# Another starting place for the low parts of the weights, and another pair of distances in each feed-forward stage

## The chip, the core and the metric

The kernel runs on one core of a Trainium2 chip. The metric is the device time of one execution in microseconds (us). A core has TensorE (PE in the profile; its weight loads have a row of their own, PEld), VectorE (DVE), ScalarE (ACT), GpSimd (POOL) and SyncE (SP, which here only issues DMAs). A matmul holds a block of 128x128 weights in the array and streams the other operand past it; the load of the next block runs while the present operand streams. Both are read from SBUF, which has 128 partitions. In each partition, every operand is a run of 4-byte elements that begins at some address.

## What is computed

A decoder trunk of two layers on 256 tokens of width 1024, all in 32-bit floats:

```python
h = x
for layer in range(2):
    if layer == 1:
        shared_kv = shared_moba_kv(h, positions, kv_norm_g, w_kv, k_norm_g)
    h = h + 0.5 * swiglu(rms_norm(h, ffn1_norm_g[layer]), w_gate, w_up, w_down)   # stages a and c
    hn = rms_norm(h, mix_norm_g[layer])
    # layer 0: convolution module beside attention to a memory
    # layer 1: causal attention over shared_kv beside attention to a memory
    ...
    h = h + jnp.concatenate([primary, mem_out], axis=-1) @ w_o[layer]
    h = h + 0.5 * swiglu(rms_norm(h, ffn2_norm_g[layer]), w_gate2, w_up2, w_down2)  # stages b and d

def swiglu(x, w_gate, w_up, w_down):
    return (jax.nn.silu(x @ w_gate) * (x @ w_up)) @ w_down
```

The inner width of a feed-forward stage is 2816, that is 22 tiles of 128.

## The kernel before

Activations are held transposed: features on the partitions, the 256 tokens along the free dimension. For the sake of precision each 32-bit operand is split into a high part, which TensorE takes at full speed, and the low part that is left over. A product is then three: high by high, high by low and low by high.

Weights come from HBM in chunks of 128x2048, each worked in two halves of 128x1024 (eight blocks of 128x128). `half_hi` gives each half two buffers out of a ring of four: ScalarE copies the high part into `wh`, VectorE writes the low part into `wl` (the raw weights less the high part). Each `wh` and each `wl` buffer is 1024 elements long.

The activations of a stage lie in one buffer from `y_tiles(name, at)`. It is 128 elements longer than its content, and the content begins `at` elements into it. For each of the eight feature tiles k the high part (256 elements) is followed by the low part (256). The numbers `at` come from the table `Y_AT` and are 8 where nothing else is said.

A feed-forward stage (`ffn`, four calls: a, b, c, d) has two halves. The **gate half** goes over 22 tiles j, and for each over gate and up and over eight k (tiles named `ag`, `au`, `bg` and so on): 352 pairs of matmuls. The **down half** goes over eight output tiles m and 22 k (tiles `ao`, `bo` and so on). Its moving operand is `hs`, the product of the gate half, in high and low parts laid out as in `y`. Both use `mm2`, a pair of matmuls on one k: a **wide** one with the block of `wh` as its weights, which streams high and low part together (512 columns), and a **narrow** one with the block of `wl`, which streams the high part alone (256 columns). The last output tile of the down half uses `mm3`, three narrow matmuls per k (`wh`, `wh` again, `wl`), so a down half has 7 x 22 = 154 pairs and 66 single narrow ones. In stage a the first two tiles j are taken together: per k four wide matmuls, then four narrow ones, eight such blocks in all.

While the wide matmul of k streams, the next load is that block of `wl`; while the narrow one streams, the next load is the `wh` block of the following k. What is called **distance** here is the start of the streaming operand less the start of the block being loaded, in elements of 4 bytes, counted modulo 32 (128 bytes). As the buffers are laid out, `y`, `wh` and `wl` buffers all begin at the same place modulo 128 bytes, and `hs` begins 8 elements further. All steps inside them (128 elements from block to block, 512 from k to k) are multiples of 32. So a `y` that begins 8 elements into its buffer has distance 8 from `wh` and from `wl`, and `hs` has distance 8 from both too.

Other products in the program have other distances. The projections `kv`, `A`, `B`, `C`, `M` and `mkv` stream weights 512 columns wide past activations with `at` 0 (distance 0). `Q` does so with 256 columns (distance 0). `mqJ`, `b0J`, `b1J` and `b2J` stream weights 256 columns wide past `cy`, which has `at` 16 (distance 16). `obo` streams `cat` 256 columns wide past blocks of `wh` and `wl` (distance 8).

Of the kernel before, what the change touches and what calls it, by code (L numbers as in the profile page):

```python
# [10 lines left out]
F32R = mybir.dt.float32r  # L11
# [6 lines left out]
P = 128  # L18
DM = 1024
KD = DM // P  # L20
SEQ = 256
NT = SEQ // P
DFF = 2816
KF = DFF // P
# [14 lines left out]
HC = 1024  # L39
# [69 lines left out]
S_A, S_B, S_BIAS, S_F, S_G = 0, PW, 2 * PW, 3 * PW, 3 * PW + P  # L109
NSPEC = 4 * PW  # L110

Y_AT = {"ay0": 0, "by0": 0, "cy0": 16}

@with_exitstack
def tile_kernel(ctx: ExitStack, tc: tile.TileContext, w, xT, memT, pos, vec, hg, const, wave, bias, taps, out):
    nc = tc.nc
    cp = ctx.enter_context(tc.tile_pool(name="cp", bufs=1))
    wp = ctx.enter_context(tc.tile_pool(name="wp", bufs=3))
# [32 lines left out]
    nc.vector.memset(mhalf, -0.5)  # L151


    state = {"chunk": 0, "half": 0, "raw": None, "order": "", "last": {}, "between": None, "made": []}

    def behind(i, other):
        tc.add_manual_dep(i.ins, other.ins.name,
# [20 lines left out]
    def tables(func):  # L178

        behind(A(nc.scalar.activation(warm, onec, func)), state["func"])  # L180
# [10 lines left out]
    def load_chunk(n):  # L191
        if n == 0:
            return raw0
        raw = wp.tile([P, CH], F32, name=f"raw{n}", tag="raw", bufs=3)
        if n < 3:
            nc.sync.dma_start(raw[:, :HC], w[n][:, :HC])
            state["sync"] = nc.sync.dma_start(raw[:, HC:], w[n][:, HC:])
        else:
            state["sync"] = nc.sync.dma_start(raw, w[n])
        return raw  # L200

    def half_hi():
        n, h = state["chunk"], state["half"]
        if h == 0:
            state["raw"] = load_chunk(n)
        raw = state["raw"][:, h * HC:(h + 1) * HC]
        wh = wp.tile([P, HC], F32R, name=f"wh{n}_{h}", tag="wh", bufs=4)
        wl = wp.tile([P, HC], F32R, name=f"wl{n}_{h}", tag="wl", bufs=4)
        state["chunk"], state["half"] = (n, 1) if h == 0 else (n + 1, 0)
        q = HC // 2 if n < 2 else HC  # L210
        parts = [slice(c, c + q) for c in range(0, HC, q)]

        def hi(s):
            state["act"] = nc.scalar.activation(wh[:, s], raw[:, s], AF.Copy)  # L214
            return state["act"]

        def lo(s):
            state["dve"] = nc.vector.tensor_tensor(wl[:, s], raw[:, s], wh[:, s].bitcast(F32), op=ALU.subtract)  # L218
            return state["dve"]
        return wh, wl, parts, hi, lo  # L220

    def half_chunk():
        if state["made"]:
            return state["made"].pop(0)
        wh, wl, parts, hi, lo = half_hi()
        for s in parts:
            hi(s)
            lo(s)
        return wh, wl

    def tiles_of(n_half):
        for n in range(n_half):
            wh, wl = half_chunk()
            for i in range(8):
                yield wh[:, i * P:(i + 1) * P], wl[:, i * P:(i + 1) * P]

    def mm3(o, wt, y, k, first, last, **kw):
        h, l = wt
        i = mmul(o, h, y[:, k, 0], start=first, stop=False, **kw)
        mmul(o, h, y[:, k, 1], start=False, stop=False, **kw)  # L240
        mmul(o, l, y[:, k, 0], start=False, stop=last, **kw)
        return i

    def mm2(o, wt, y, k, first, last, turn=None):

        h, l = wt
        a = mmul(o, h, y[:, k].rearrange("p a s -> p (a s)"), start=first, stop=False)
        if turn is not None:
            state["between"] = a
            turn()  # L250
            last_turn, state["between"] = state["between"], None
        b = mmul(o[:, :SEQ], l, y[:, k, 0], start=False, stop=last)
        if turn is not None:
            behind(b, last_turn)
# [9 lines left out]
    def both_halves(name, o, tag):  # L264

        c = tp.tile([P, SEQ], F32, name=name + "c", tag="cvq")
        nc.scalar.activation(c, o[:, SEQ:], AF.Copy)
        a = tp.tile([P, SEQ], F32, name=name, tag=tag)
        nc.vector.tensor_tensor(a, o[:, :SEQ], c, op=ALU.add)
        return a  # L270
# [7 lines left out]
    def psum(name, tag="mm", bufs=4):  # L278
        return ps.tile([P, 512], F32, name=name, tag=tag, bufs=bufs)


    def y_tiles(name, at=8):

        n = KD * 2 * SEQ
        y = yp.tile([P, n + P], F32R, name=name, tag="y")
        return y[:, at:at + n].rearrange("p (k h s) -> p k h s", k=KD, h=2)

    def scaled_split(y, src, k, g, on_dve=False):

        yh, yl = y[:, :, 0], y[:, :, 1]  # L290
        if on_dve:
            h = nc.vector.tensor_scalar(yh[:, k], src, vt[:, g + k:g + k + 1], None, op0=ALU.mult)
        else:
            h = nc.scalar.activation(yh[:, k], src, AF.Copy, scale=vt[:, g + k:g + k + 1])
        return h, nc.vector.scalar_tensor_tensor(yl[:, k], src, vt[:, g + k:g + k + 1], yh[:, k].bitcast(F32),
                                                 op0=ALU.mult, op1=ALU.subtract)

    def square_sum(name, acc, src, first, adder=nc.gpsimd):
        if first:
            nc.scalar.activation(acc, src, AF.Square)  # L300
        else:
            sq = tp.tile([P, SEQ], F32, name=name, tag="sq")
            nc.scalar.activation(sq, src, AF.Square)
            adder.tensor_tensor(acc, acc, sq, op=ALU.add)
# [32 lines left out]
    def new_acc(name):  # L337
        return tp.tile([P, SEQ], F32, name=name, tag="acc")

    def ffn(name, y, acc, nexts, store=False, hook=None, after=None, hook_down=None, r=None, plan=None):  # L340


        plan = plan or {}
        rows_at = [j for (j, _, _), what in plan.items() if what == "rows"]
        hs = cp.tile([P, KF, 2, SEQ], F32R, name=name + "hs", tag="hs")
        first = acc is None
        rb = None if r is None else bcast_rows(name + "nb", r)
        halves = {}
# [22 lines left out]
        for j in range(KF):  # L371
# [4 lines left out]
            if first and j == 0:  # L376
# [21 lines left out]
                n = KD  # L398
# [9 lines left out]
            else:  # L408

                at = ("sc", 2) if first and j == 2 else ()  # L410
# [21 lines left out]
            for i in sorted(halves):  # L432
                g, h = halves.pop(i)
                if i > 1 or not rows_at:
                    g, h = both_halves(f"{name}gs{i}", g, "g"), (lambda i=i, h=h: both_halves(f"{name}h{i}", h, "h"))
                gated(i, g, h, rb)
        if after:
            tables(after)
        ys = [y_tiles(f"{name}y{i}", Y_AT.get(f"{name}y{i}", 8)) for i in range(len(nexts))]
        acc = new_acc(name + "acc")  # L440
        it = tiles_of(KD * KF // 8)
        for m in range(KD):
            po = psum(f"{name}o{m}")
            if hook_down:
                with tc.issue_after(state["act"].ins):
                    hook_down(m)

            both_sums = m < KD - 1
            for k in range(KF):
                if both_sums:  # L450
                    mm2(po, next(it), hs, k, k == 0, k == KF - 1)
                else:
                    mm3(po[:, :SEQ], next(it), hs, k, k == 0, k == KF - 1)
            if both_sums:
                d = both_halves(f"{name}d{m}", po, "g")
                nc.vector.scalar_tensor_tensor(d, d, 0.5, rb, op0=ALU.mult, op1=ALU.mult)
            else:
                d = tp.tile([P, SEQ], F32, name=f"{name}d{m}", tag="g")
                nc.vector.scalar_tensor_tensor(d, po[:, :SEQ], 0.5, rb, op0=ALU.mult, op1=ALU.mult)
            nc.vector.tensor_tensor(x[:, m], d, x[:, m], op=ALU.add)  # L460
            if store:
                nc.sync.dma_start(out[m], x[:, m])
                continue
            for yy, g in zip(ys, nexts):
                state["ends"] = scaled_split(yy, x[:, m], m, g)
            square_sum(f"{name}q{m}", acc, x[:, m], m == 0)
        return ys, acc

    def heads_norm(name, t, n):
# [78 lines left out]
    def room_of(tile_):  # L548

        taken = [0]  # L550

        def place(*shape):

            n = int(np.prod(shape))
            taken[0] += n
            assert taken[0] <= tile_.shape[1], taken
            piece = tile_[:, taken[0] - n:taken[0]]
            if len(shape) == 1:
                return piece
            names = [f"d{i}" for i in range(len(shape))]  # L560
            return piece.rearrange(f"p ({' '.join(names)}) -> p {' '.join(names)}", **dict(zip(names, shape)))
        return place
# [143 lines left out]
        square_sum(f"{name}q{m}", acc, x[:, m], m == 0)  # L706


    y = y_tiles("y0")
    for k in range(KD):  # L710
        scaled_split(y, x[:, k], k, V_FFN1, k % 2 == 0)
    kv0 = []
# [416 lines left out]
        steps[name]()  # L1129
    state["order"] = ""  # L1130
    o, cat = late["o"], late["cat"]
    ys = y_tiles("oay")
    acc = new_acc("oaacc")
    it = tiles_of(CC - FIRST_CAT)
    for m in range(KD):
        for k in range(FIRST_CAT, CC):
            mm3(o[m], next(it), cat, k, False, k == CC - 1, skip_group_check=True)
        out_end(m, o, ys, acc, V_FFN2, "oa")
    y = ys
    (ykv, y), acc = ffn("b", y, acc, (V_KV, V_FFN1 + KD), plan={(2, "g", 5): "rows"})  # L1140


# [11 lines left out]
                    plan={(2 + i, "g", 4): turn for i, turn in enumerate(turns)})  # L1154
    qT = cp.tile([P, KD, SEQ], F32, name="q1T", tag="t8k")
    cat = y_tiles("cat1")
    ys = y_tiles("oby")
    place = room_of(cp.tile([P, KF * 2 * SEQ], F32, name="room", tag="hs"))
    steps, step = stepper()

# [186 lines left out]
    y, acc = ys, sums  # L1347
# [162 lines left out]
```

## Time and profile before

| what | value |
|---|---|
| median of three runs | 958.7 us (958.36 to 959.63) |
| the profiled execution, its time | 958.8 us |
| its span, first to last instruction | 956.8 us |
| PE busy | 950.2 us, 99% of the span |
| DVE, ACT, POOL busy | 75%, 59%, 11% |
| HBM read | 172.15 MB, 181 GB/s over the span |
| granted TensorE clock | 1.000 |

The span is one execution as the profiler recorded it; its time holds 2.0 us more that lie around the span. A row of the timeline gives the start, the duration, engine, line, operation and operands (out<-in). Matmuls overlap in the array, so the duration of one (some 0.39 or 0.28 us) is longer than the step from its start to the start of the next, and it is these steps that add up to the span. Rows that run into each other without a break and have the same operands are merged, with their count behind an x.

### The profile page before, as it was taken

The page shows a single profiled execution, that of the slowest core. Times are in us where ns is not written, and L with a number is a line of the kernel's source. Part 1 is how long each engine was busy: PE and PEld are TensorE (multiplying, and loading weights), DVE is VectorE, ACT ScalarE, POOL GpSimd, SP SyncE. Part 2 cuts the span into 40 slices and gives each one's busy share as a digit, 9 for nine tenths or more (in the row PEclk, how much of TensorE's full clock was granted, in tenths as well). Part 3 has the DMA queues.
Part 4 walks back from the last instruction along what each step waited for, and adds up shares of the span by engine and source line. Part 5 has one row for each costly group of instructions (what it writes and reads, how often), then busy time and mean ns, then how long its engine had stood idle before and what let it go on. Part 6 is the DMA issues. An engine that isn't in the chain of part 4 may idle for free.

```text
span 956.8 us, 15067 instructions
## 1 busy us (share of the span) xinstructions
PE 950.2 (99%) x5699; PEld 833.0 (87%) x5699; DVE 719.1 (75%) x1243; ACT 561.8 (59%) x1026; POOL 103.1 (11%) x101
## 2 busy tenths in 40 slices
PE   9999999999999999999999999999999999999998
PEld 6888888888789888888988888888997998888887
DVE  7888877767887877767767777767779578777663
ACT  6676666554566665555556665555548666556442
POOL 0122000112223000001123000000134120000000
PEclk9999999999999999999999999999999999999999
DMA  8755555554334655555555455555542245555560
GB/s 326 272 197 181 176 190 205 178 182 170 133 132 166 216 191 179 195 199 176 192 194 188 176 187 205 181 183 202 187 177 79 99 176 188 208 177 184 199 215 19
DMA packets 26936, 174.16 MB, mean 182 GB/s; under 512 B 3376, under 2 KB 5136, under 8 KB 6512
## 3 DMA queue, kind: packets, MB, share of 16 engines
q1 hardware_dynamic: 26576, 173.04, 51.4%
q8 instruction: 44, 0.72, 0.3%
q14 instruction: 28, 0.23, 0.1%
q10 hardware_dynamic: 288, 0.17, 0.1%
HBM read 172.15 MB, written 1.05 MB: 181 GB/s over the span
## 4 chain that ended last, share of the span: by engine, by line
PE 96%; DVE 3%; ACT 0%; POOL 0%; issue 0%; ACTq 0%
PE ag L183 6%; PE au L183 6%; PE do L183 6%; PE co L183 6%; PE bo L183 6%; PE ao L183 6%; PE bg L183 6%; PE dg L183 6%; PE cg L183 6%; PE cu L183 6%; PE bu L183 6%; PE du L183 6%; PE kv L183 3%; PE obo L183 2%; PE oao L183 2%; PE A L183 1%
## 5 line engine op out<-in xcount | busy, mean ns | idle before, releaser
L214 ACT ACTIVATE wh<-raw 128x1024 fp32r<-128x1024 f32 (+1 forms) x326 | 341.8, 1050 | 339.5 <-PE dg L183 26.8
L218 DVE TENSOR_TENSOR wl<-raw,wh 128x1024 fp32r<-128x1024 f32 (+1 forms) x326 | 396.5, 1218 | 178.2 <-ACT wh L214 176.9
L183 PE MATMUL ag<-y,wh 128*128 128x512 f32 x176 | 63.7, 396 | 0.0
L183 PE MATMUL au<-y,wh 128*128 128x512 f32 x176 | 63.2, 392 | 0.0
L183 PE MATMUL bg<-oay,wh 128*128 128x512 f32 x176 | 62.4, 391 | 0.0
L183 PE MATMUL dg<-oby,wh 128*128 128x512 f32 x176 | 62.4, 391 | 0.0
L183 PE MATMUL bu<-oay,wh 128*128 128x512 f32 x176 | 62.2, 390 | 0.0
L183 PE MATMUL du<-oby,wh 128*128 128x512 f32 x176 | 62.2, 390 | 0.0
L183 PE MATMUL cg<-by,wh 128*128 128x512 f32 x176 | 62.2, 391 | 0.0
L183 PE MATMUL cu<-by,wh 128*128 128x512 f32 x176 | 62.1, 391 | 0.0
L183 PE MATMUL bo<-bhs,wh 128*128 128x512 f32 (+1 forms) x198 | 61.1, 367 | 0.0
L183 PE MATMUL ao<-ahs,wh 128*128 128x512 f32 (+1 forms) x198 | 61.1, 367 | 0.0
L183 PE MATMUL co<-chs,wh 128*128 128x512 f32 (+1 forms) x198 | 61.1, 367 | 0.0
L183 PE MATMUL do<-dhs,wh 128*128 128x512 f32 (+1 forms) x198 | 61.1, 367 | 0.0
L183 PE MATMUL cg<-by,wl 128*128 128x256 f32 x176 | 49.8, 283 | 0.0
L183 PE MATMUL bg<-oay,wl 128*128 128x256 f32 x176 | 49.7, 282 | 0.0
L183 PE MATMUL dg<-oby,wl 128*128 128x256 f32 x176 | 49.7, 282 | 0.0
L183 PE MATMUL du<-oby,wl 128*128 128x256 f32 x176 | 49.6, 282 | 0.0
L183 PE MATMUL cu<-by,wl 128*128 128x256 f32 x176 | 49.6, 282 | 0.0
L183 PE MATMUL bu<-oay,wl 128*128 128x256 f32 x176 | 49.6, 282 | 0.0
L183 PE MATMUL ag<-y,wl 128*128 128x256 f32 x176 | 49.6, 284 | 0.0
L183 PE MATMUL au<-y,wl 128*128 128x256 f32 x176 | 49.4, 283 | 0.0
(948 smaller groups left out, 2309.6 us busy)
## 6 DMA issues: line engine op xcount, KB each, us to landing
raw<-in_w SPq DMA_DIRECT2D x158, 1024.0 KB, 4.8
raw<-in_w SPq DMA_DIRECT2D x5, 512.0 KB, 8.2
mT<-in_memT SPq DMA_DIRECT2D x1, 1024.0 KB, 8.3
out<-x SPq DMA_DIRECT2D x8, 128.0 KB, 1.8
raw<-in_w SPq DMA_DIRECT2D x2, 256.0 KB, 4.0
x<-in_xT SPq DMA_DIRECT2D x1, 512.0 KB, 6.6
spec<-in_bias SPq DMA_DIRECT2D x1, 384.0 KB, 9.8
tapw<-in_taps SPq DMA_DIRECT2D x1, 288.0 KB, 9.1
```

What stands on the lines that cost most here:

```text
L183: return in_order("P", nc.tensor.matmul(*a, **k))
L214: state["act"] = nc.scalar.activation(wh[:, s], raw[:, s], AF.Copy)
L218: state["dve"] = nc.vector.tensor_tensor(wl[:, s], raw[:, s], wh[:, s].bitcast(F32), op=ALU.subtract)
```

## The change

Three things are done. Each `wl` buffer becomes 32 elements longer, and the low part begins `state["wl_at"]` elements into it. That number is set at the start of a stage's gate half, set again at the start of its down half, and is 0 outside. Each `hs` buffer becomes 128 elements longer, and its content begins at a place from `HS_AT`. And the activations of stages a, b, c and d get other places `at`.

```diff
-Y_AT = {"ay0": 0, "by0": 0, "cy0": 16}
+Y_AT = {"ay0": 0, "by0": 0, "by1": 8, "cy0": 16}
+HS_AT = {'a': 24, 'b': 0, 'c': 8, 'd': 0}
+WL_AT = {'a': (16, 24), 'b': (16, 8), 'c': (16, 8), 'd': (16, 24)}
...
-        wl = wp.tile([P, HC], F32R, name=f"wl{n}_{h}", tag="wl", bufs=4)
+        wl = wp.tile([P, HC + 32], F32R, name=f"wl{n}_{h}", tag="wl", bufs=4)[:, state["wl_at"]:state["wl_at"] + HC]
...
     def ffn(name, y, acc, nexts, store=False, hook=None, after=None, hook_down=None, r=None, plan=None):
+        state["wl_at"] = WL_AT[name][0]
...
-        hs = cp.tile([P, KF, 2, SEQ], F32R, name=name + "hs", tag="hs")
+        n, at = KF * 2 * SEQ, HS_AT[name]
+        hs = cp.tile([P, n + P], F32R, name=name + "hs", tag="hs")
+        hs = hs[:, at:at + n].rearrange("p (k h s) -> p k h s", k=KF, h=2)
...
         acc = new_acc(name + "acc")
+        state["wl_at"] = WL_AT[name][1]
         it = tiles_of(KD * KF // 8)
...
+        state["wl_at"] = 0
         return ys, acc
...
-    y = y_tiles("y0")
+    y = y_tiles("y0", 0)
...
-    ys = y_tiles("oay")
+    ys = y_tiles("oay", 16)
...
-    ys = y_tiles("oby")
+    ys = y_tiles("oby", 24)
```

No instruction is added, removed or moved: on each of the five engines the same instructions stand in the same order, with the same shapes. What differs is where operands begin. The buffers of `wl` now begin 4224 bytes apart, which is again a multiple of 128 bytes, so the beginnings modulo 128 bytes follow from the tables alone. Distances, as the narrow matmul meets them (to the next `wh`) and the wide one (to the next `wl`):

| half | pairs | before: narrow, wide | after: narrow, wide |
|---|---|---|---|
| gate a | 352, of them 32 in the eight blocks of four | 8, 8 | 0, 16 |
| gate b | 352 | 8, 8 | 16, 0 |
| gate c | 352 | 8, 8 | 8, 24 |
| gate d | 352 | 8, 8 | 24, 8 (the first 32 pairs: 24, 24) |
| down a | 154 and 66 single | 8, 8 | 0, 8 |
| down b | 154 and 66 single | 8, 8 | 8, 0 |
| down c | 154 and 66 single | 8, 8 | 16, 8 |
| down d | 154 and 66 single | 8, 8 | 8, 16 |

The first 32 pairs of stage d take halves of weights that were made ahead, while `wl_at` was still 0. The projection `mkv0`, which stands inside the gate half of stage a, is made with `wl_at` 16; its 16 matmuls that stream `wl` get distance 16 where they had 0. All other products keep their distances.

More of the change, by code (lines that the diff above doesn't have):

```diff
@@ L151, in tile_kernel @@
     nc.vector.memset(mhalf, -0.5)
-    state = {"chunk": 0, "half": 0, "raw": None, "order": "", "last": {}, "between": None, "made": []}
+    state = {"chunk": 0, "half": 0, "raw": None, "order": "", "last": {}, "between": None, "made": [], "wl_at": 0}
     def behind(i, other):
```

## The prediction

> **What bounds the kernel now.** I read the page first: the busy times, then the chain that ended last.
>
> ```profile
> span 956.8 us, 15067 instructions
> PE 950.2 (99%) x5699; PEld 833.0 (87%) x5699; DVE 719.1 (75%) x1243; ACT 561.8 (59%) x1026; POOL 103.1 (11%) x101
> PEclk9999999999999999999999999999999999999999
> PE 96%; DVE 3%; ACT 0%; POOL 0%; issue 0%; ACTq 0%
> L218 DVE TENSOR_TENSOR wl<-raw,wh 128x1024 fp32r<-128x1024 f32 (+1 forms) x326 | 396.5, 1218 | 178.2 <-ACT wh L214 176.9
> ```
>
> PE is busy nearly all the time, at full granted clock, and 96% of the chain is PE: a nanosecond saved or lost on a matmul is saved or lost at the end. DVE, which makes the low parts, still idles 178.2 us, so a somewhat faster PE would not run dry. The groups of matmuls, shapes kept apart, tell where that time is:
>
> ```profile
> L183 PE MATMUL bg<-oay,wh 128*128 128x512 f32 x176 | 62.4, 391 | 0.0
> L183 PE MATMUL bg<-oay,wl 128*128 128x256 f32 x176 | 49.7, 282 | 0.0
> L183 PE MATMUL bo<-bhs,wh 128*128 128x512 f32 x154 | 53.4, 392 | 0.0
> ```
>
> No idle time stands before any of them. With gate and up, four gate halves hold 1408 pairs of a wide and a narrow matmul, four down halves 616. What a pair takes is read from starts on the timeline. First, which load runs beside which matmul:
>
> ```profile
> 300.14 0.39 PE L183 MATMUL bg<-oay,wh 128*128 128x512 f32 x1
> 300.36 0.28 PE L183 MATMUL bg<-oay,wl 128*128 128x256 f32 x1
> 300.14 0.19 PEld L183 LDWEIGHTS bg<-oay,wl 128*128 128x128 f32 x1
> 300.37 0.19 PEld L183 LDWEIGHTS bu<-oay,wh 128*128 128x128 f32 x1
> ```
>
> The load of `wl` starts with the wide matmul, the load of the next `wh` with the narrow one. So the wide matmul lives with the distance to `wl`, the narrow one with the distance to `wh`. Now 46 pairs of a gate half and 29 of a down half, first and last start:
>
> ```profile
> 349.72 0.39 PE L183 MATMUL bu<-oay,wh 128*128 128x512 f32 x1
> ...
> 365.66 0.39 PE L183 MATMUL bu<-oay,wh 128*128 128x512 f32 x1
> 442.64 0.39 PE L183 MATMUL bo<-bhs,wh 128*128 128x512 f32 x1
> ...
> 452.69 0.39 PE L183 MATMUL bo<-bhs,wh 128*128 128x512 f32 x1
> ```
>
> 15.94 / 46 = 346.5 ns and 10.05 / 29 = 346.6 ns. `oay` and `hs` lie differently beyond 128 bytes, and the pairs agree: nothing here speaks for more than the distance modulo 128 bytes.
>
> **Does the distance matter?** The program itself holds runs of narrow matmuls alone at distances 0 (`Q`), 8 (`obo`) and 16 (`b2J`), and of wide ones at 0 (`kv`). First and last start of each:
>
> ```profile
> 227.79 0.28 PE L183 MATMUL Q<-wl,ay 128*128 128x256 f32 x1
> ...
> 230.43 0.28 PE L183 MATMUL Q<-wh,ay 128*128 128x256 f32 x1
> 755.03 0.28 PE L183 MATMUL obo<-cat,wl 128*128 128x256 f32 x1
> ...
> 760.33 0.28 PE L183 MATMUL obo<-cat,wl 128*128 128x256 f32 x1
> 719.78 0.28 PE L183 MATMUL b2J<-wl,cy 128*128 128x256 f32 x1
> ...
> 721.25 0.28 PE L183 MATMUL b2J<-wh,cy 128*128 128x256 f32 x1
> 493.76 0.62 PE L183 MATMUL kv<-wh,by 128*128 128x512 f32 x2
> ...
> 496.26 0.39 PE L183 MATMUL kv<-wl,by 128*128 128x512 f32 x1
> ```
>
> Narrow: 2.64 us over 22 steps is 120 ns at distance 0; 5.30 over 45 is 118 at 8; 1.47 over 13 is 113 at 16. Wide: 2.50 over 11 is 227 ns at 0. At 8 the wide one is what the pair leaves, 346.5 - 118 = 228.5. Higher wide rows exist too, both at distance 8: the blocks of four in stage a, and a few pairs that run late.
>
> ```profile
> 15.72 0.40 PE L183 MATMUL ag<-y,wh 128*128 128x512 f32 x1
> 16.65 0.28 PE L183 MATMUL ag<-y,wl 128*128 128x256 f32 x1
> 27.20 0.40 PE L183 MATMUL au<-y,wh 128*128 128x512 f32 x1
> 27.91 0.39 PE L183 MATMUL au<-y,wh 128*128 128x512 f32 x1
> 697.08 0.28 PE L183 MATMUL co<-chs,wl 128*128 128x256 f32 x1
> 697.20 0.28 PE L183 MATMUL mqJ<-wh,cy 128*128 128x256 f32 x1
> ```
>
> Four wide ones take 0.93 us, 233 each. Two pairs take 0.71, 355 each, which leaves 355 - 118 = 237 for the wide one. The last two rows are the only narrow step at distance 24 (`hs` streams while `cy` is loaded): 0.12 us.
>
> How far down could it go? The warm-up matmuls, with 2-byte operands, run at 8.66 us as eight of 512 columns:
>
> ```profile
> 8.66 1.90 PE L183 MATMUL pw<-busy 128*128 128x512 bf16 x8
> L183 PE MATMUL pw<-busy 128*128 128x512 bf16 x11 | 2.7, 381 | 0.0
> ```
>
> (1900 - 381) / 7 = 217 ns a step, where the wide 4-byte ones take 227 and more: some 10 ns that depend on the operands.
>
> The Trainium skill would have it otherwise. Its page "TensorE: Matmul & The Clock Gate", section "Step-by-step: what each phase is for", says that streaming operand and weight load have read ports of their own, so that loading the next weights takes no read bandwidth from the running matmul. By that rule no distance could change anything, and the sum would be 0. The trace disagrees: 120 against 113 ns for one shape. Section "Back-to-back issue gap" gives columns / 2.4 + 2.5 ns, an estimate of 216 for 512 columns, which fits the 217 of the 2-byte rows and not the 227 of the others.
>
> **The change, part by part.** Costed at nothing: the longer buffers (space alone) and the writes to other places. ScalarE writes to a `y` at 8 and at 16 take the same time, and these writes lie beside matmuls anyway.
>
> ```profile
> L294 ACT ACTIVATE oay<-x,vt 128x256 fp32r<-128x256 f32 x8 | 4.0, 502 | 1.4 <-DVE x L704 1.4
> L294 ACT ACTIVATE cy<-x,vt 128x256 fp32r<-128x256 f32 x8 | 4.0, 500 | 0.2
> ```
>
> No instruction moves, so no queue is passed and no wait is added. What is left are the steps between matmuls, all on the path. Against 118 and 228.5 at distance 8, and supposing that wide and narrow add up each by its own distance:
>
> - Narrow at 0: +2. Narrow at 16: -5. Wide at 0: -1.5. All from rows.
> - Narrow at 24: bounds 113 (lowest row) and 125 (the single step, with its rounding). I take 120, +2, what that step reads.
> - Wide at 16: no row. Bounds 227 and 237. It rises from 0 to 8, so I take the higher row that many matmuls share, 233: +4.5.
> - Wide at 24: no row, same bounds. It is as near to 0 (by the wrap at 32) as to 16: the mean of 227 and 233 is 230, +1.5.
>
> | half | working (ns) | us |
> |---|---|---|
> | gate a | 320 pairs x (2 + 4.5) | +2.08 |
> | its 8 blocks | three wide 227, one 233, three narrow 113, one 120 = 1373, before 1400 (four of 350) | -0.22 |
> | gate b | 352 x (-5 - 1.5) | -2.29 |
> | gate c | 352 x (0 + 1.5) | +0.53 |
> | gate d | 320 x 2 + 32 x 3.5 | +0.75 |
> | down a, b | 154 x 2; 154 x -1.5 | +0.31, -0.23 |
> | down c, d | 154 x -5; 154 x 4.5 | -0.77, +0.69 |
> | last output tiles | 44 x 2 + 22 x 2 - 44 x 5 - 22 x 5 | -0.20 |
> | `mkv0` | 16 x (233 - 227) | +0.10 |
>
> The sum is +0.75 us. The profiled execution took 958.8 us (span 956.8), 0.1 above the median, so the forecast is 959.5: gains and losses cancel.
>
> With every unseen step at its low end (wide at 16 and 24 227, narrow at 24 113) the rows give gate a -0.1, b -2.3, c -0.5, d -1.8, the down halves -0.9, the rest -0.2: -5.8, or 953.0. At the high end (237, 237, 125): gate a +3.2, b -2.3, c +3.0, d +2.7, the down halves +0.6: +7.2, or 966.0.
>
> **The rivals.** A measurement here tells 0.2% (1.9 us) from no change.
>
> *Slower: the wide step climbs with distance.* At 16 and 24 a wide matmul settles at 235 or more, as the four-blocks and the late pairs do already. That is 0.88 us per ns over some 880 matmuls. With 228.5 in both places the sum would be -2.1, so it is slower by 0.2% from 233 on and reaches 966 at 237. For it: at one and the same distance 8 the wide step takes 228.5 in most pairs, but 233 in the four-blocks and 237 in the late pairs, so higher steps are within reach. Against: the long runs of pairs at 8 keep to 228.5.
>
> *Faster: the wide step doesn't care, and narrow at 24 is like 16.* This is the low end, 953. For it: wide moves only 1.5 between 0 and 8, narrow 7 over its rows. It decides where wide stays at 228.5 or below with narrow at 24 no more than 120. Against: the one step at 24 reads 0.12.
>
> *No effect.* The differences between those runs come from their form (weights streaming or standing), not from distance: 958.8. `obo` and `Q` differ in form and by 2 ns only; but `Q` and `b2J` have the same form and differ by 7.
>
> *Pairs lock as a whole.* Pairs take 346 or 355 and little between. If a half settles on one step of some 7 ns up or down, each gate half moves by 352 x 7 = 2.5 us at once. It widens every case more than it names one.
>
> **How the numbers follow.** The cancelling sum gets 0.43, of it 0.28 within 0.2% and 0.15 slower, since it leans up. The climbing wide step gets 0.25, the faster case 0.24, no effect 0.08. That makes 0.24 faster, 0.36 the same, 0.40 slower. The range takes both ends of the unseen steps and a little for locking: 952 to 967.
>
> **What would show it.** After the change, steps in gate b should read 113 and 227 (340 a pair, against 346.5), in down c 113 and 228.5, in gate a narrow 120. The halves to look at are those with unseen steps: gate a and down d (wide at 16), gate c (wide at 24), gate d (narrow at 24). Wrong would be the whole way of adding if gate b didn't gain some 2 us, if the wide step answered to the distance of `wh`, or if pairs at one distance took two different times for long stretches. The busy time of DVE and ACT should stay as it is.

## The result, and the profile after

The changed kernel takes 965.64 us (median of three runs, 964.56 to 965.82), the kernel before 958.7. The ratio is 1.0067, with a 95% interval of 1.0044 to 1.0090: slower by 0.7%. The profiled execution has a span of 963.9 us, 7.1 more than before. Its page, the lines on busy times, clock, chain and the making of low parts:

```profile
span 963.9 us, 15067 instructions
PE 956.6 (99%) x5699; PEld 832.1 (86%) x5699; DVE 719.0 (75%) x1243; ACT 562.2 (58%) x1026; POOL 103.3 (11%) x101
PEclk9999999999999999999999999999999999999999
PE 95%; DVE 3%; DMA 1%; ACT 1%; SPq 0%; issue 0%; ACTq 0%
L220 DVE TENSOR_TENSOR wl<-raw,wh 128x1024 fp32r<-128x1024 f32 (+1 forms) x326 | 396.5, 1218 | 182.9 <-ACT wh L216 181.5
```

PE is busy 6.4 us longer at the same clock, while the work of DVE and ACT is what it was (719.1 and 561.8 us before). But for the first microseconds (below), no engine began to wait; the matmuls themselves stand further apart. By halves, from the first start in one to the first start in the next (for a down half to its own last start), in us:

| part | before | after | change | forecast |
|---|---|---|---|---|
| gate a | 138.67 | 140.92 | +2.25 | +1.96 |
| down a | 61.03 | 61.59 | +0.55 | +0.40 |
| gate b | 123.78 | 123.11 | -0.67 | -2.29 |
| down b | 61.03 | 61.45 | +0.41 | -0.19 |
| gate c | 122.83 | 124.09 | +1.26 | +0.53 |
| down c | 61.03 | 61.81 | +0.78 | -0.99 |
| gate d | 126.95 | 128.12 | +1.17 | +0.75 |
| down d | 61.03 | 61.56 | +0.53 | +0.58 |
| all else | 200.4 | 201.2 | +0.8 | 0 |

(The forecast's terms for the last output tiles and for `mkv0` stand with their halves.) Of gate a's 2.25 us some 1.2 fall before 28.6 us, in the first 120 matmuls of the stage, where the loads had just begun and PE waited once for a low part; the rest of the half took 117.68 us where it took 116.66, +1.0.

```profile
10.77 0.38 PE L185 MATMUL ag<-y,wl 128*128 128x256 f32 x1 [0.57 <-DVE wl L220]
```

The telling rows are in gates b and d. On the timeline, gate and up take turns of eight pairs. The first wide start of a turn, three turns in a row, in stage b and then in stage d of the changed kernel:

```profile
343.11 0.40 PE L185 MATMUL bg<-oay,wh 128*128 128x512 f32 x1
...
345.89 0.39 PE L185 MATMUL bu<-oay,wh 128*128 128x512 f32 x1
...
348.62 0.40 PE L185 MATMUL bg<-oay,wh 128*128 128x512 f32 x1
...
825.41 0.40 PE L185 MATMUL dg<-oby,wh 128*128 128x512 f32 x1
...
828.24 0.39 PE L185 MATMUL du<-oby,wh 128*128 128x512 f32 x1
...
831.01 0.40 PE L185 MATMUL dg<-oby,wh 128*128 128x512 f32 x1
```

In stage b eight pairs of gate take 2.78 us, 347.5 ns a pair, and eight of up 2.73, 341. In stage d it is 2.83 and 2.77: 353.8 and 346.3. Gate and up of a stage have the same distances modulo 128 bytes. What they don't share is the buffer: the ring has four `wl` buffers, gate gets two of them and up the other two, and since buffers lie 4224 bytes apart, every second one is 128 bytes off modulo 256. Sorted by the distance modulo 256 bytes (64 elements; counted so, `hs` begins 40 elements further than the other buffers), means over all pairs of a class, the trace says:

| half | narrow, wide | ns | narrow, wide | ns |
|---|---|---|---|---|
| gate b | 16, 32 | 347.9 | 16, 0 | 341.6 |
| gate d | 24, 40 | 353.4 | 24, 8 | 346.6 |
| gate c | 8, 24 | 351.9 | 8, 56 | 348.9 |
| gate a | 0, 48 | 348.6 | 0, 16 | 351.6 |
| down a | 0, 8 | 353.4 | 0, 40 | 346.8 |
| down b | 40, 32 | 351.1 | 40, 0 | 346.9 |

In these halves buffers 256 bytes apart fall into the same class and agree to 0.6 ns. (In down c and d the two classes lie within 3 ns of each other.) Something else moved too. The queries keep their places, yet their narrow matmuls, 113 ns apart before, take longer. First and last of 18 steps in `mqJ` of the changed kernel:

```profile
702.18 0.28 PE L185 MATMUL mqJ<-wl,cy 128*128 128x256 f32 x1
...
704.30 0.28 PE L185 MATMUL mqJ<-wl,cy 128*128 128x256 f32 x1
```

2.12 / 18 = 118 ns. Half of their `wl` buffers are 128 bytes off as well.

### The profile page after: what moved, and what is told of

It reads as the page before. It is cut to its first block, busy times and chain, and to the rows that moved or that the text cites. A ratio compares the mean times of both kernels' runs of the same rounds, so it can differ in the third digit from the quotient of the medians.

```text
span 963.9 us, 15067 instructions
## 1 busy us (share of the span) xinstructions
PE 956.6 (99%) x5699; PEld 832.1 (86%) x5699; DVE 719.0 (75%) x1243; ACT 562.2 (58%) x1026; POOL 103.3 (11%) x101
## 4 chain that ended last, share of the span: by engine, by line
PE 95%; DVE 3%; DMA 1%; ACT 1%; SPq 0%; issue 0%; ACTq 0%
PE dg L185 6%; PE cg L185 6%; PE co L185 6%; PE ao L185 6%; PE do L185 6%; PE bo L185 6%; PE cu L185 6%; PE bg L185 6%; PE du L185 6%; PE bu L185 6%; PE au L185 6%; PE ag L185 6%; PE kv L185 3%; PE obo L185 2%; PE oao L185 2%; PE M L185 1%
## 5 line engine op out<-in xcount | busy, mean ns | idle before, releaser
L185 PE MATMUL co<-chs,wl 128*128 128x256 f32 x176 | 49.4, 281 | 0.0
L185 PE MATMUL bo<-bhs,wl 128*128 128x256 f32 x176 | 49.2, 281 | 0.0
```

Of the source, the lines that this page charges most:

```text
L185: return in_order("P", nc.tensor.matmul(*a, **k))
```

## The experiments

### The length alone

`wl` buffers 32 elements longer, all starting places as before (the `hs` buffers keep their 128 more elements, here and in all runs below):

```diff
-        wl = wp.tile([P, HC], F32R, name=f"wl{n}_{h}", tag="wl", bufs=4)
+        wl = wp.tile([P, HC + 32], F32R, name=f"wl{n}_{h}", tag="wl", bufs=4)
```

> The kernel before with nothing changed but the length of the wl buffers (1056 elements instead of 1024); every starting place is as before. Theory 256: the step of a matmul depends on the distance modulo 256 bytes (64 elements). The longer buffers put every second wl buffer 128 bytes off, so that of gate and up one keeps the pair of distances (8, 8) and takes 346.7 ns as before, while the other gets (8, 40) and takes some 4 to 7 ns more or less; in the down halves it changes every eight pairs between (40, 40) and (40, 8). At 5 ns more that is 704 and 308 pairs, +5 us: 961 to 965 (or 953 to 957 if the new pair is the better one). The queries b0J to b2J no longer run at 113 ns throughout. Theory 128 (as predicted): only the distance modulo 128 bytes counts, nothing changes: 958.7, all pairs 346.7.

963.31 us against 958.53, ratio 1.0051 (1.0036 to 1.0066). So 4.8 us of the loss come from the length alone, with not one starting place changed inside a buffer. Three turns of stage b:

```profile
342.19 0.40 PE L185 MATMUL bg<-oay,wh 128*128 128x512 f32 x1
...
344.99 0.40 PE L185 MATMUL bu<-oay,wh 128*128 128x512 f32 x1
...
347.77 0.40 PE L185 MATMUL bg<-oay,wh 128*128 128x512 f32 x1
```

2.80 and 2.78 us, where 2.77 would be 346.7 ns a pair. By classes gate b has 349.5 ns at (8, 40) and 348.2 at (8, 8); the down halves b to d 349.9 at (40, 8) and 346.8 at (40, 40). The new pairs cost 3 ns, less than the 5 expected, but the old pair (8, 8), unchanged, lost 1.5 as well; it runs in turns with the other. All else took 0.85 us longer.

### Spaced by a multiple of 256 bytes

The changed kernel, with `HC + 64` in place of `HC + 32`:

> The changed kernel with wl buffers 1088 elements long, so that they begin a multiple of 256 bytes apart. Theory 256: gate and up of a stage become alike, each at the step that one of the two had in the changed kernel at the same pair modulo 64 elements: gate a 348.5 ns (0, 48), b 341.5 (16, 0), c 348.9 (8, 56), d 346.6 (24, 8); down a 346.7 (0, 40), b 351.1 (40, 32), c 352.5 (48, 40), d 349.2 (40, 16); the queries return to 113 ns. Against 346.7 that is +0.6, -1.8, +0.8, 0, 0, +0.7, +0.9, +0.4: +1.5 us, 960.2. Theory 128: the distances modulo 128 bytes are those of the changed kernel, so it stays at 965.6, with gate and up as different as they are. Theory of the climbing wide step: at 128-byte distances 16 and 24 gate a, c and down d stay at 350 or more: 965.

961.07 us against 958.53, ratio 1.0027 (1.0018 to 1.0037). Of the loss of 6.9 us 2.5 are left, though all distances modulo 128 bytes are those of the changed kernel. That leaves the prediction's modulo no room, and the climbing wide step, which would have kept 965, falls with it. Gate and up are alike now in each stage. 48 pairs of stage b, gate and up together:

```profile
341.32 0.39 PE L185 MATMUL bg<-oay,wh 128*128 128x512 f32 x1
...
357.64 0.39 PE L185 MATMUL bg<-oay,wh 128*128 128x512 f32 x1
```

16.32 / 48 = 340.0 ns. The gate halves came near what was expected: a 347.1, b 340.4, c 348.9, d 346.7. Of the down halves b (351.2), c (353.3) and d (348.4) did within 1 ns, but a took 351.7 where 346.7 was expected for (0, 40): in the changed kernel that pair ran in turns with (0, 8), here it runs alone. Of the queries `b0J` to `b2J` are back at 113 to 114 ns, `mqJ` stays at 117, and all else is within 0.1 us of before. Those 117 are a mean of two steps at one place: the first 36 matmuls of `mqJ` stand 118 ns apart; then come four small ones (`rqp`), and behind them it is 113, as in the kernel before.

### The pair (16, 0) everywhere

```diff
-Y_AT = {"ay0": 0, "by0": 0, "by1": 8, "cy0": 16}
-HS_AT = {'a': 24, 'b': 0, 'c': 8, 'd': 0}
-WL_AT = {'a': (16, 24), 'b': (16, 8), 'c': (16, 8), 'd': (16, 24)}
+Y_AT = {'ay0': 0, 'by0': 0, 'by1': 16, 'cy0': 16}
+HS_AT = {'a': 40, 'b': 40, 'c': 40, 'd': 40}
+WL_AT = {'a': (16, 16), 'b': (16, 16), 'c': (16, 16), 'd': (16, 16)}
...
-        wl = wp.tile([P, HC + 32], F32R, name=f"wl{n}_{h}", tag="wl", bufs=4)
+        wl = wp.tile([P, HC + 64], F32R, name=f"wl{n}_{h}", tag="wl", bufs=4)
...
-    y = y_tiles("y0", 0)
+    y = y_tiles("y0", 16)
...
-    ys = y_tiles("oby", 24)
+    ys = y_tiles("oby", 16)
```

Beside this, the halves made ahead for stage d get `wl_at` 16, and `proj` works with `wl_at` 0.

> All eight halves get the pair (16, 0) modulo 64 elements, with wl buffers of 1088 elements; weights made ahead for stage d get their place too, and mkv0 keeps place 0. Theory 256: every pair takes the 341.5 ns that the up half of stage b showed: 2024 pairs x -5.2 ns = -10.5 us, 948. If the pair locks fully at its shortest step, 340.0: 945. Theory 128 with wide and narrow adding up: 118 - 5 and 228.5 - 1.5, 340 a pair, 945. Theory that the step is a matter of form and not of places: 958.7.

946.5 us against 958.53, ratio 0.9873 (0.9858 to 0.9887): 1.3% faster than the kernel before, with the same instructions in the same order. The span is 943.8 us. All eight halves average 340.1 to 341.3 ns a pair (gate c begins with 33 pairs at 350 before it comes to 340); a down half takes 60.04 us where it took 61.03, gate b 121.58 where it took 123.78. The down half of stage a, first and last of 29 pairs:

```profile
149.86 0.39 PE L185 MATMUL ao<-ahs,wh 128*128 128x512 f32 x1
...
159.75 0.39 PE L185 MATMUL ao<-ahs,wh 128*128 128x512 f32 x1
```

9.89 / 29 = 341 ns. This version beats both kernels. It doesn't tell 256 bytes from 128: adding up modulo 128 bytes expected 945 as well.

### A survey of other pairs

The same `wl` buffers of 1088 elements, eight other pairs (stage c's activations begin at 16):

```diff
-HS_AT = {'a': 24, 'b': 0, 'c': 8, 'd': 0}
-WL_AT = {'a': (16, 24), 'b': (16, 8), 'c': (16, 8), 'd': (16, 24)}
+HS_AT = {'a': 24, 'b': 8, 'c': 48, 'd': 16}
+WL_AT = {'a': (48, 0), 'b': (32, 16), 'c': (0, 24), 'd': (32, 16)}
...
-    y = y_tiles("y0", 0)
+    y = y_tiles("y0", 48)
...
-    ys = y_tiles("oby", 24)
+    ys = y_tiles("oby", 48)
...
```

> Other pairs modulo 64 elements, one for each half, to see which rule they follow; gate a (48, 0), b (16, 48), c (16, 16), d (48, 16); down a (0, 0), b (48, 32), c (24, 0), d (56, 40). Theory 256 with wide and narrow adding up: narrow 113 at 16 and at 48, wide 227 at 0: gate a 340; b, c and d 113 + 228 to 235 = 341 to 348; down a 120 + 227 = 347; c 118 + 227 = 345; b and d 345 to 355. Theory 256 without adding up (the pair of distances decides as a whole): values off these by 5 ns or more in at least two halves. Theory 128: gate a is the same as (16, 0), and c and d are the same, each to 1 ns.

967.5 us (one run). The pairs took: (48, 0) 346.3, (16, 48) 353.0, (16, 16) 353.2, (48, 16) 353.3, (0, 0) 346.8, (48, 32) 352.8, (24, 0) 348.9, (56, 40) 352.8. Adding up wide and narrow steps from single runs gives 341 to 348 for the second to the fourth, and misses these by 5 ns or more. For the first it gives 340, and the 346.3 there is a mean of two steps. 24 pairs of gate a early in the half, and 48 late in it:

```profile
48.02 0.39 PE L185 MATMUL ag<-y,wh 128*128 128x512 f32 x1
...
56.19 0.39 PE L185 MATMUL au<-y,wh 128*128 128x512 f32 x1
...
118.90 0.40 PE L185 MATMUL au<-y,wh 128*128 128x512 f32 x1
...
135.70 0.40 PE L185 MATMUL au<-y,wh 128*128 128x512 f32 x1
```

8.17 / 24 = 340 and 16.80 / 48 = 350 ns, at one pair of distances. So (48, 0) reaches the step of (16, 0), to which it is equal modulo 128 bytes, and (16, 16) and (48, 16) are alike: these would fit 128 bytes as well. (48, 32), also equal to (16, 0) modulo 128 bytes, would not: after some 40 pairs it keeps to 353.3, which no half at (16, 0) did.

### The same distances at other addresses

Everything in (16, 0), with `wh`, `wl`, `y` and `hs` 24 elements further:

```diff
-        wh = wp.tile([P, HC], F32R, name=f"wh{n}_{h}", tag="wh", bufs=4)
+        wh = wp.tile([P, HC + 64], F32R, name=f"wh{n}_{h}", tag="wh", bufs=4)[:, 24:24 + HC]
...
```

> The kernel with (16, 0) in all eight halves, and wh, wl, y and hs of the halves all moved 24 elements (96 bytes) further, so that in every half the distances stay and the addresses do not. Theory distance: the pairs stay at 340 ns, a gate half at 120.8 to 121.6 us (stages b, c), a down half at 60.0. Theory address: it was the place modulo 256 bytes of one operand alone that made them fast; then pairs go to 346 to 353, a down half to 61.0 to 62.1 us. Products outside the feed-forward stages get other distances by this move (their wh moves, their activations and wl do not), so the whole time can be some us longer and is not what is compared.

949.9 us (one run). Its span, 948.1 us, is 4.3 longer than that of the version before: 1.7 us lie in the products outside the feed-forward stages, 1.2 in gate a and 1.5 in down a. Gates b, c and d and the down halves b, c and d are at 340.1 to 341.0 ns, like those of the version before: there the address as such does not count, the distance does. But the down half of stage a was something neither theory had. It keeps to 350.0 ns in all of its pairs. 28 pairs of it, and 29 of stage b with the same addresses modulo 256 bytes and the same distances:

```profile
149.90 0.40 PE L185 MATMUL ao<-ahs,wh 128*128 128x512 f32 x1
...
159.71 0.40 PE L185 MATMUL ao<-ahs,wh 128*128 128x512 f32 x1
...
424.77 0.40 PE L185 MATMUL bo<-bhs,wh 128*128 128x512 f32 x1
...
434.65 0.39 PE L185 MATMUL bo<-bhs,wh 128*128 128x512 f32 x1
```

9.81 / 28 = 350 ns, 9.88 / 29 = 341. One pair of distances can run at two steady steps.

### Run again

The shifted kernel and the one with (16, 0) everywhere, each once more:

> The same kernel as the shifted one, run once more. There the pairs of the down half of stage a kept to 350.0 ns (61.56 us) while those of b, c and d with the same pair of distances kept to 340.2 (60.04 us). Theory chance entry: which of the two steps a half settles on is a matter of the moment, and another execution shows 60.04 in a or 61.5 in another half. Theory determined entry: the instructions ahead of the half decide, and the second execution repeats 61.56, 60.04, 60.04, 60.04 to within 0.1 us.

> The kernel with (16, 0) in all eight halves, run once more with a profile. Theory chance entry: one of its down halves, all at 60.04 us before, comes out at 61.5. Theory determined entry: all four at 60.04 again, to within 0.1 us.

The shifted kernel repeated 61.56, 60.04, 60.04, 60.04 to the last digit, the other one 60.04 four times. So in these runs the step on which a half settles was not chance. Where stage a went to the longer one can be seen in the gate half of the first shifted run. Two small matmuls (`spc`) stand between a wide matmul and its narrow one there. Ten pairs ahead of them, and ten behind:

```profile
110.22 0.39 PE L185 MATMUL ag<-y,wh 128*128 128x512 f32 x1
...
113.62 0.39 PE L185 MATMUL au<-y,wh 128*128 128x512 f32 x1
113.84 0.40 PE L185 MATMUL spc<-tapr,rootr 96*128 96x256 f32 x2
...
114.20 0.39 PE L185 MATMUL au<-y,wh 128*128 128x512 f32 x1
...
117.70 0.40 PE L185 MATMUL au<-y,wh 128*128 128x512 f32 x1
```

3.40 / 10 = 340 and 3.50 / 10 = 350 ns, and 350 it stays to the last pair of the down half. In the kernel that isn't shifted the same two `spc` stand at the same spot, and behind them the pairs are back at 340 after two steps of 351 and 345. So an interruption can tip the pairs from one step to the other without any change of distances. Which property of it decides was not tried.

### Around (16, 0)

Other places in the same buffers, again one pair of distances for each half:

> Pairs around (16, 0) modulo 64 elements, one for each half: gate a (12, 0), b (20, 0), c (16, 4), d (16, 60); down a (16, 56), b (16, 8), c (8, 0), d (32, 0). Theory broad: within 4 elements (16 bytes) of (16, 0) the pair still locks at 340 ns, so gates b and c take 121.6 and 120.8 us as with (16, 0). Theory sharp: 4 elements off cost as much as 8, 346 or more, gates 123 us or more. Theory of the prediction (wide and narrow add up, each by its own distance): c of the down halves 118 + 227 = 345, d 113 to 120 + 227 = 340 to 347, a and b 113 + 228.5 to 231 = 342 to 344, that is 59.9 to 60.8 us where (40, 40) took 61.0.

960.2 us (one run). (16, 60) locks at 340.2 ns, and (16, 4) at 353; (20, 0) takes 346.8 and (12, 0) 349.8; (16, 56) 346.8, (16, 8) 348.8, (8, 0) 344.9, (32, 0) 352.0. 44 pairs of stage d at (16, 60), and 42 of stage c at (16, 4):

```profile
799.69 0.39 PE L185 MATMUL dg<-oby,wh 128*128 128x512 f32 x1
...
814.65 0.39 PE L185 MATMUL du<-oby,wh 128*128 128x512 f32 x1
...
559.94 0.40 PE L185 MATMUL cg<-by,wh 128*128 128x512 f32 x1
...
574.78 0.40 PE L185 MATMUL cu<-by,wh 128*128 128x512 f32 x1
```

14.96 / 44 = 340 and 14.84 / 42 = 353 ns. From (16, 0) to (16, 4), by 16 bytes, the step goes from the best to nearly the worst; 16 bytes the other way it stays. So neither theory holds on both sides. Each of these pairs was seen in one half of one run, and as (16, 0) has a second step, they may have others too. The way of the prediction, adding up, gives (8, 0) as 345 but misses (16, 56), (16, 8) and (32, 0) by some 3 ns or more.

### The narrow matmuls of the output projections

`cat0` and `cat1` at 16 in place of 8, all else with (16, 0):

```diff
-            late["cat"] = y_tiles("cat0")
+            late["cat"] = y_tiles("cat0", 16)
...
-    cat = y_tiles("cat1")
+    cat = y_tiles("cat1", 16)
```

> The kernel with (16, 0) in all eight halves, and cat0 and cat1 moved from place 8 to place 16, so that the narrow matmuls alone of the two output projections (oao, obo) stand at distance 16. If distance 16 gives narrow matmuls 113 ns there as in the queries: 380 x -4 ns = -1.5 us, 945.0 where the same kernel with cat at 8 took 946.5. If they depend on more than that distance (they load wh, wh again, wl): 946.5, no change.

946.12 us against 959.36, ratio to the kernel before 0.9862 (0.9846 to 0.9879). That overlaps the 0.9873 (0.9858 to 0.9887) without this edit, and the steps say why: `oao` 117.8 ns where it had 116.7, `obo` 117.3 where it had 117.2. The 113 of the queries did not carry over to matmuls that load `wh`, `wh` and `wl` in another order. Nor are they firm: `b0J`, whose places this edit leaves alone, takes 117.8 here where it had 113.3.

## Why the prediction was right in its range and short in its size

965.6 lies within 952 to 967, and slower had the largest chance, 0.40. The forecast, 959.5, was 6 us too low. That the range held is in part luck: its upper end, 966.0, came from a wide step of 237 and a narrow one of 125, while 4.8 us of the loss came from the spacing of buffers, which the sum had at nothing. By two of the prediction's own signs the whole way of adding was wrong: gate b didn't gain some 2 us, and pairs at one distance took two different times for long stretches.

*What bounds the kernel* held: each nanosecond between matmuls came out at the end, in both directions, and DVE and ACT did not move.

*The step that failed* is the first one: "nothing here speaks for more than the distance modulo 128 bytes". It rested on the agreement of `oay` (346.5) and `hs` (346.6). Modulo 256 bytes these are two different pairs, (8, 8) and (40, 40), which happen to run alike. The step counted the new spacing of 4224 bytes for nothing. The length alone was worth 4.8 us; spacing by a multiple of 256 bytes took the loss from 6.9 us to 2.5. In the profiled execution with the length alone, whose span is 5.3 us longer, 0.85 us lie outside the feed-forward stages, where the forecast had 0.

*The terms on their own rows.* Gate b, -2.29 forecast, was -0.67 with half of its buffers at another distance, and -2.20 once they were spaced by a multiple of 256 bytes: there 113 and 227 do make 340. Down b and c, -0.19 and -0.99 forecast, came to +0.71 and +1.09 in the same run. Modulo 256 bytes their pairs are (40, 32) and (48, 40), not (8, 0) and (16, 8). And (16, 8) itself, 341.5 by the prediction's rows, took 348.8.

*Adding up* holds at (16, 0), at (8, 0) with 345 against 344.9 and at (0, 0) with 347 against 346.8, and not in general: (16, 16), (16, 48), (16, 8). And a pair may have two steps, 340 and 350. Steps from runs of narrow matmuls alone don't give the step of a mixture, and they have two values themselves: `mqJ` stood at 118 and at 113 with its places modulo 256 bytes as before.

*The guessed steps.* Gate d with narrow at 24 was forecast at 348.5 by one single row; at (24, 8) it is 346.7, so its gain of 0 in the spaced kernel was missed by 0.7 us. Gate a and down d, whose wide step was taken at 233, came out near the forecast (+2.25 for +1.96, +0.53 for +0.58), but not for that reason: their classes are a mixture, and half of gate a's loss lies in its first matmuls.

*The rivals.* The slower one had the right side and not the mechanism: with the distances modulo 128 bytes left where they are, its time went from 965.6 to 961.1. (Nor does its own rate of 0.88 us per ns reach 966 at 237, but 964.2; the 966.0 of the high end needs the narrow 125 too.) The faster one is out: of the eight halves only gate b gained. Locking as a whole, named only to widen the range, came nearest: many long stretches keep to 340, 347, 350 or 353 ns. No effect, as the rule of the Trainium skill would have it (page "TensorE: Matmul & The Clock Gate", section "Step-by-step: what each phase is for"), is out: places alone moved the time from 946.5 to 965.6 us. That it is the two reads which hinder each other is not shown.

## What to carry to other kernels

In this kernel, bound by a stream of 4-byte matmuls, the place of the streaming operand against the next weights was worth 1.3%, for nothing but padding. When padding the buffers of a ring, keep them at the same place modulo 256 bytes: here the gain of one place was lost in every second buffer. Measure pairs of distances in the very mixture of matmuls that will run, and read the steps along the stretch and not only their mean: single runs of one shape did not add up, and a mean can hide two steps.

## What the runs showed of the hardware

- The step between matmuls depends on the places of operands beyond 128 bytes. `wl` buffers 4224 bytes apart in place of 4096, with every place modulo 128 bytes kept, cost 4.8 us; and in gate b of the changed kernel (16, 32) took 347.9 ns and (16, 0) 341.6 in turns, but 340.4 in all turns once the buffers lay 4352 apart. With 4352, buffers an odd and those an even multiple of 256 bytes off agree to 0.5 ns in gates b to d and in all down halves.
- 16 bytes can count: (16, 0) and (16, 60) keep to 340 ns, (16, 4) to 353, the last two seen in one half each.
- Many long stretches keep to a mean step of 340.0, 346.7, 350.0 or 353.3 ns; others to 344.5, 348.9 or 352.
- One pair of distances can have two steps: 340 and 350 ns at (16, 0) and at (48, 0), 118 and 113 for the narrow matmuls of `mqJ`. A few small matmuls between the pairs can tip them from one to the other, and both shifted runs settled alike.
